# Matmul with batch norm over rows: x cast in GpSimd DMAs and transposed on VectorE, column tiles finished one after another

One core of a Trainium2 chip. The metric is the time of one execution in device microseconds; the profile's span runs from the first to the last instruction and is some 2 us shorter.

## The reference

```python
x: (16, 512, 1024) fp32     weight: (1024, 768) fp32     gamma, beta: (768,)
y = np.matmul(x, weight)                        # 8192 x 768
mean = np.mean(y, axis=(0, 1)); var = np.var(y, axis=(0, 1))
return gamma * (y - mean) / np.sqrt(var + eps) + beta
```

The statistics of a column need all 8192 rows of it, so no element of a column can be finished before its last row is multiplied. But columns do not depend on one another: that is what the change uses.

## The kernel before

Rows come in 16 chunks of 512, columns in six tiles of 128, the contraction in eight pieces of 128. y^T of all chunks stays in SBUF as bf16.

```python
for mt in range(M_T):                       # 16 chunks
    x_sb = xpool.tile([P, M_SUB, K], f32)
    nc.sync.dma_start(x_sb, ...)            # 2 MB, rows of 4 KB
    nc.scalar.copy(x_bf, x_sb)              # cast to bf16
    for kt in range(K_T):                   # 32 transposes of 128x128 on TensorE
        for ms in range(M_SUB):
            nc.tensor.transpose(psum_t[:, ms, :], x_bf[:, ms, kt*P:(kt+1)*P], ident)
        nc.scalar.copy(xT_sb[:, kt, :], psum_t)
    for nt in range(N_T):
        for kt in range(K_T):
            nc.tensor.matmul(py, w_sb[:, kt, nt*P:(nt+1)*P], xT_sb[:, kt, :], ...)
        nc.vector.bn_stats(stats_sb[:, nt, mt, :], py)
        nc.vector.tensor_copy(yT_sb[:, nt, m0:m0 + M_CHUNK], py)
# ... aggregate statistics, scale and shift of all 768 columns ...
for mt in range(M_T):
    for nt in range(N_T):
        nc.scalar.activation(yn, yT_sb[...], Identity, bias=shift, scale=scale)
        for ms in range(M_SUB):
            nc.tensor.transpose(opsum[:, ms, :], yn[:, ms*P:(ms+1)*P], ident)
        nc.vector.tensor_copy(o_sb, opsum)
        nc.sync.dma_start(out[...], o_sb)   # 256 KB, rows of 512 bytes, three buffers
```

## Time and profile before

| | before |
|---|---|
| median of 3 runs before the prediction | 353.72 us (353.66 to 353.81) |
| start, TensorE without work | 0 to 20 us |
| matmuls and input transposes | 20 to 236 us, TensorE clock 1.00 |
| output stage | 240 to 352 us, clock 0.50, DMA share 0.79 |

The slices behind this table are shown in the prediction; the last two rows are these stretches, with the columns of the prediction's table of stretches:

```profile
20.00:236.00 216.00, 203.99 (x1256) 104.89 (x1280) 123.60 (x195) 121.97 (x145) 0.00 (x0) 1.00 0.38 138
...
240.00:352.00 112.00, 56.23 (x384) 40.04 (x384) 66.26 (x96) 75.65 (x96) 0.00 (x0) 0.50 0.79 226
```

In the line of slices each digit is the busy share of one fortieth of the span in tenths. In a group, the figures after the bar are total busy time and the mean of one in ns, then the idle time of the engine just ahead of them and what ended it. A 512-column matmul is recorded with 380 ns, but the next starts 216 ns after it. Costs of matmuls are therefore read from start to start.

### The profile page before, as it was taken

To read this page: it belongs to the slowest core of one execution; us is meant where nothing else is said; L and a number is where in the kernel's file an instruction comes from. 1 tells how busy PE (TensorE), PEld (TensorE's weight loads), DVE (VectorE), ACT (ScalarE), POOL (GpSimd) and SP (SyncE) were. 2 spreads that over 40 slices of the span, in tenths; PEclk is the share of its full clock that TensorE was granted. 3 is DMA by queue.
4 is the path that set the end of the run, shared out by engine and by line. 5 is a ranking of instruction groups with operands and counts; after the bars stand their busy time and mean duration, and the time that the engine had idled before them with its cause. 6 is when DMAs were issued, how large, how long until landed. Compare 5 with 4: busy or idle time off the path is not lost.

```text
span 352.2 us, 4346 instructions
## 1 busy us (share of the span) xinstructions
PE 260.5 (74%) x1640; PEld 144.9 (41%) x1664; DVE 196.1 (56%) x300; ACT 203.1 (58%) x243; POOL 0.7 (0%) x6
## 2 busy tenths in 40 slices
PE   0059999999999999999999999984554555455542
PEld 0034554544544544544544544533333334333331
DVE  0306556556565565465475475495664666566653
ACT  1196835835835736736736633607775777577751
POOL 0000000000000000000000000000000000000000
PEclk9999999999999999999999999995555555555555
DMA  7999563363372362462460000004886888688867
GB/s 288 409 342 325 187 238 102 138 239 98 143 240 81 159 238 72 168 238 50 190 238 2 0 2 1 2 0 114 245 245 199 243 243 255 180 249 240 254 194 208
DMA packets 61925, 62.16 MB, mean 176 GB/s; under 512 B 3536, under 2 KB 52688, under 8 KB 61904
## 3 DMA queue, kind: packets, MB, share of 16 engines
q1 hardware_dynamic: 61904, 61.88, 53.6%
q8 instruction: 13, 0.21, 0.3%
q14 instruction: 8, 0.07, 0.1%
HBM read 36.71 MB, written 25.17 MB: 176 GB/s over the span
## 4 chain that ended last, share of the span: by engine, by line
PE 47%; DMA 27%; ACT 13%; DVE 10%; issue 2%; DVEq 0%; SPq 0%; ACTq 0%
PE py L87 42%; DMA out_dram<-o_sb 22%; ACT xT_sb L82 11%; DVE o_sb L134 7%; PE psum_t L77 5%; DMA x_sb<-in_x_dram 4%; ACT x_bf L71 2%; DVE yT_sb L95 1%; DVE stats_sb L94 1%; DVE mv_sb L99 1%; DVEq L134 0%; ACT yn L124 0%; PE opsum L132 0%; SPq L55 0%; ACT tmp L114 0%
## 5 line engine op out<-in xcount | busy, mean ns | idle before, releaser
L87 PE MATMUL py<-xT_sb,w_sb 128*128 128x512 bf16 x744 | 178.8, 380 | 1.6 <-ACT xT_sb L82 1.1
L94 DVE BATCH_NORM_STATS2 stats_sb<-py 128x6 f32<-128x512 f32 x96 | 66.8, 696 | 97.4 <-PE py L87 97.3
L82 ACT COPY xT_sb<-psum_t 128x512 bf16<-128x512 bf16 x128 | 67.9, 586 | 86.8 <-PE psum_t L77 86.8
L87 PEld LDWEIGHTS <-w_sb 128*128 128x128 bf16 x768 | 74.6, 98 | 80.0 <-issue 5.0
L132 PE MATMUL opsum<-ident,yn 128*128 128x128 bf16 x384 | 56.2, 300 | 54.7 <-DVE o_sb L134 49.3
L124 ACT ACTIVATE yn<-yT_sb,shift_sb,scale_sb 128x512 bf16<-128x512 bf16 x96 | 76.2, 811 | 30.2 <-PE opsum L132 26.4
L134 DVE CAST o_sb<-opsum 128x512 f32<-128x512 bf16 x96 | 66.3, 691 | 43.2 <-DMA out_dram<-o_sb 31.3
L77 PE MATMUL psum_t<-ident,x_bf 128*128 128x128 bf16 x512 | 47.4, 220 | 30.4 <-ACT x_bf L71 20.4
L132 PEld LDWEIGHTS <-yn 128*128 128x128 bf16 x384 | 40.0, 137 | 71.1 <-issue 64.9
L71 ACT CAST x_bf<-x_sb 128x4096 bf16<-128x4096 f32 x16 | 57.7, 3608 | 14.7 <-DMA x_sb<-in_x_dram 14.7
L95 DVE CAST yT_sb<-py 128x512 bf16<-128x512 f32 x96 | 64.6, 673 | 0.0
L77 PEld LDWEIGHTS <-x_bf 128*128 128x128 bf16 x512 | 37.6, 98 | 51.0 <-issue 26.9
L57 DVE CAST w_sb<-w_tmp 128x6144 bf16<-128x6144 f32 x1 | 3.4, 3359 | 10.8 <-DMA w_tmp<-in_weight_dram 10.8
L114 ACT ACTIVATE tmp<-mv_sb,eps_sb 128x6 f32<-128x6 f32 x1 | 0.3, 299 | 9.3 <-DVE mv_sb L99 9.3
L99 DVE BATCH_NORM_AGGREGATE mv_sb<-stats_sb 128x2 f32<-128x96 f32 x6 | 3.5, 578 | 0.0
L71 ACT ACT_TABLE_LOAD x1 | 1.3, 1283 | 0.7 <-PEq L155 0.7
L114 ACT ACT_TABLE_LOAD x1 | 1.3, 1283 | 0.0
L113 DVE MEMSET eps_sb<- 128x1 f32 x1 | 0.1, 59 | 0.8 <-PEq L155 0.8
L115 DVE RECIPROCAL scale_sb<-tmp 128x6 f32<-128x6 f32 x1 | 0.2, 191 | 0.4 <-ACT tmp L114 0.4
masks.py:199 POOL TENSOR_SCALAR_AFFINE_SELECT ident<-ident 128x128 bf16<-128x128 bf16 x1 | 0.3, 292 | 0.1
L116 DVE TENSOR_TENSOR scale_sb<-scale_sb,gamma_sb 128x6 f32<-128x6 f32 x1 | 0.2, 167 | 0.1
masks.py:197 POOL MEMSET ident<- 128x128 bf16 x1 | 0.2, 205 | 0.3 <-POOLq L155 0.3
(6 smaller groups left out, 0.7 us busy)
## 6 DMA issues: line engine op xcount, KB each, us to landing
x_sb<-in_x_dram SPq DMA_DIRECT2D x16, 2048.0 KB, 7.8
out_dram<-o_sb SPq DMA_DIRECT2D x96, 256.0 KB, 2.4
w_tmp<-in_weight_dram SPq DMA_DIRECT2D x1, 3072.0 KB, 10.9
gamma_sb<-in_gamma_dram SPq DMA_DIRECT2D x6, 0.5 KB, 7.6
beta_sb<-in_beta_dram SPq DMA_DIRECT2D x6, 0.5 KB, 7.2
```

Of the source, the lines that this page charges most:

```text
L57: nc.vector.tensor_copy(w_sb, w_tmp)
L71: nc.scalar.copy(x_bf, x_sb)
L77: nc.tensor.transpose(psum_t[:, ms, :], x_bf[:, ms, kt * P:(kt + 1) * P], ident,)
L82: nc.scalar.copy(xT_sb[:, kt, :], psum_t)
L87: nc.tensor.matmul(py, w_sb[:, kt, nt * P:(nt + 1) * P], xT_sb[:, kt, :], start=(kt == 0), stop=(kt == K_T - 1),)
L94: nc.vector.bn_stats(stats_sb[:, nt, mt, :], py)
L95: nc.vector.tensor_copy(yT_sb[:, nt, m0:m0 + M_CHUNK], py)
L99: nc.vector.bn_aggr(mv_sb[:, nt, :], stats_sb[:, nt, :, :])
L114: nc.scalar.activation(tmp, var, mybir.ActivationFunctionType.Sqrt, bias=eps_sb, scale=1.0)
L124: nc.scalar.activation(yn, yT_sb[:, nt, m0:m0 + M_CHUNK], mybir.ActivationFunctionType.Identity, bias=shift_sb[:, nt:nt + 1], scale=scale_ ...
L132: nc.tensor.transpose(opsum[:, ms, :], yn[:, ms * P:(ms + 1) * P], ident)
L134: nc.vector.tensor_copy(o_sb, opsum)
```

## The change

The intent is to take everything but matmuls off TensorE's path, and to write output while TensorE still multiplies:

- x comes through casting DMAs as bf16 (of the weights one half too, the other half as fp32 through the hardware queue). VectorE transposes 32x32 blocks of *pairs* of bf16, taken as one fp32 word; the rows of the weights are permuted so that the contraction still matches. A matmul then reads every second bf16 of the pairs.
- x^T of chunks 4 to 15 stays in SBUF. All six column tiles are computed for chunks 0 to 3, three tiles for the rest; these three are then complete, and their output runs beside the matmuls of tile 3, and so on. These three are stored together, in rows of 1.5 KB; each later tile alone, in rows of 512 bytes.
- Output transposes stand one behind each matmul, what is left of a bank just before its copy. Evacuation of y moves from VectorE to ScalarE, normalization from ScalarE to VectorE.
- 26 dummy matmuls run at the start, the schedule is laid out by planned times in the code, and each engine's order is pinned to it.

```diff
-        nc.sync.dma_start(x_sb, x_flat[...])
-        nc.scalar.copy(x_bf, x_sb)
-                nc.tensor.transpose(psum_t[:, ms, :], x_bf[...], ident)
-            nc.scalar.copy(xT_sb[:, kt, :], psum_t)
+        for i in range(4):                                  # load_x, 256 rows
+            seq(nc.gpsimd.dma_start(x_bf[32 * i:32 * i + 32], rows[:, :, KQ * i:KQ * (i + 1)]))
+        src = xs[q].rearrange("p t k -> p (t k)").bitcast(f32)   # turn_x
...
+        seq(nc.vector.transpose(dst[:, half, :, jw0:jw1], src[:, :, jw0:jw1]))
...
+                seq(nc.tensor.matmul(                       # mm: eight per unit
+                    y_ps, w_sb[:, jw, e, nt * P:(nt + 1) * P], xT[c][:, jw, :, e], ...))
+                if turns:
+                    turn_one()                              # one output transpose
...
+    for c in range(2, C):
+        for nt in range(NT if c < EARLY else GA):           # EARLY = 4, GA = 3
+            unit(nt, c, MM_US)
+    at(pe + 1.9, finish, ga)
+    outputs(ga, pe + 6.0, 2.24, 2, 2)
+    for nt in range(GA, NT):
+        for c in range(EARLY, C):
+            unit(nt, c, MM_US + (1.05 if nt == GA else 0.35))
+        at(pe + 1.9, finish, [nt])
+        outputs([nt], pe + 7.0, 2.3 if nt < NT - 1 else 1.0, 8, 1)
```

The cuts leave out the pools, the start with chunks 0 and 1 in halves, the statistics, and the rest of the schedule.

## The prediction

> **What bounds the kernel now.** I read the page first, then a table of stretches, then the tensor engine's own timeline in one steady stretch. From the page, the slices, the chain of work that ended last, and four groups:
>
> ```profile
> span 352.2 us, 4346 instructions
> ...
> PE   0059999999999999999999999984554555455542
> ...
> PEclk9999999999999999999999999995555555555555
> DMA  7999563363372362462460000004886888688867
> ...
> PE 47%; DMA 27%; ACT 13%; DVE 10%; issue 2%; DVEq 0%; SPq 0%; ACTq 0%
> ...
> L87 PE MATMUL py<-xT_sb,w_sb 128*128 128x512 bf16 x744 | 178.8, 380 | 1.6 <-ACT xT_sb L82 1.1
> ...
> L82 ACT COPY xT_sb<-psum_t 128x512 bf16<-128x512 bf16 x128 | 67.9, 586 | 86.8 <-PE psum_t L77 86.8
> ...
> L134 DVE CAST o_sb<-opsum 128x512 f32<-128x512 bf16 x96 | 66.3, 691 | 43.2 <-DMA out_dram<-o_sb 31.3
> ...
> out_dram<-o_sb SPq DMA_DIRECT2D x96, 256.0 KB, 2.4
> ```
>
> There are three stages. For 20 us (slices 1 and 2) the tensor engine (PE) waits for data. Until about 236 us it is over 90% busy at full clock while DMA is used by a third and falls to 0. Then comes a stage at half clock in which DMA is 80% busy and PE half: the writing of the output. The stages follow each other because the statistics need all of y before any output can be normalized. The table of stretches puts numbers on this:
>
> ```profile
> 2.00:12.00 10.00, 0.00 (x0) 0.00 (x0) 0.38 (x1) 0.01 (x1) 0.00 (x0) 1.00 1.00 381
> 12.00:20.00 8.00, 0.00 (x0) 0.00 (x0) 2.98 (x1) 3.31 (x1) 0.00 (x0) 1.00 1.02 410
> ...
> 245.00:300.00 55.00, 29.08 (x200) 20.91 (x199) 34.50 (x50) 39.78 (x51) 0.00 (x0) 0.50 0.82 236
> ```
>
> After the length come the busy times of PE, weight loads, VectorE, ScalarE and GpSimd, then granted clock, DMA share and GB/s. Loads run at 381 to 410 GB/s with DMA full; stores of 512-byte rows do 236 GB/s at a share of 0.82, so about 288 if the queue never ran dry. It runs dry because only three output buffers circulate (31.3 us of waits of L134 on the store).
>
> The PE timeline between 100 and 128 us gives the costs:
>
> ```profile
> 106.95 9.22 PE L87 MATMUL py<-xT_sb,w_sb 128*128 128x512 bf16 x42 [0.18 <-ACT xT_sb L82]
> 116.02 0.61 PE L77 MATMUL psum_t<-ident,x_bf 128*128 128x128 bf16 x8
> 117.13 0.38 PE L77 MATMUL psum_t<-ident,x_bf 128*128 128x128 bf16 x4 [0.51 <-ACT xT_sb L82]
> ```
>
> A 512-column matmul costs (9.22 - 0.38)/41 = 0.2156 us, start to start (the 380 ns of the group is latency). A transpose costs (0.61 - 0.38)/4 = 0.0575 us. A chunk of 512 rows takes 116.02 - 102.67 = 13.35 us: 48 matmuls 10.35, 32 transposes 1.84, the remaining 1.2 waits for ScalarE's copies of x^T. So 768 matmuls are 165.6 us that nothing here removes; about 187 us of the span are start, input transposes, waits, and the output stage.
>
> **What the Trainium skill says.**
> - "DMA: Bandwidth & Descriptors", section "SWDGE vs HWDGE vs iDMA": a casting DMA must come from GpSimd, and its descriptors are written by software there. The kernel before has only hardware queues, so its trace shows no rate for this. It is the largest unknown.
> - "SBUF — State Buffer", section "SBUF: two separate sides": a VectorE operation in a two-port mode locks GpSimd out, and such DMAs starve. Not visible before. The change seems written with this in mind: while x loads, VectorE does transposes and statistics from PSUM; the normalizations from SBUF to SBUF come after the last load.
> - "TensorE: Matmul & The Clock Gate", section "Part 4: PE-mode transpose": transposes do not count as activity for the clock. The trace agrees: 0.50 granted in the stage that has only transposes, 1.00 before it.
> - "Vector Engine (DVE) Microarchitecture Reference", section "3.8 The reshape front-end and per-opcode configuration": the 32x32 transpose passes one element per cycle and lane. No run here shows it yet.
>
> **The change part by part.**
>
> *Loads.* x arrives as bf16 through 128 GpSimd DMAs, four per 256 rows, in 1 KB reads and 512-byte writes. Removed: 16 casts of 3.6 us on ScalarE. I assume 385 GB/s read (the low end of 381 to 410), so 2.7 us per 256 rows. Two words of bf16 are treated as one fp32, and VectorE transposes 32x32 blocks of such pairs: 32 transposes of 1024 words. Statistics over 512 elements take 0.65 us here, a 6-element operation 0.17, so I estimate 0.17 + 2 x 0.48 = 1.1 to 1.2 us each, 38 us in all. That takes 512 transposes (29 us) off PE and 128 copies (68 us) off ScalarE. VectorE also loses 96 casts (65 us), which move to ScalarE as copies of about 0.57.
>
> *Order on PE*, as the built program has it: 26 dummy matmuls, chunks 0 and 1 with half-width pieces, all six column tiles for chunks 0 to 3, three tiles for the rest; then the statistics of those three are complete, and their output work (192 transposes) goes between the matmuls of tile 3, and so on. x^T stays in SBUF for this. Of 384 output transposes, 312 stand before the last matmul, and 72 after it (8 of tile 4, 64 of tile 5).
>
> *The sum, in span time:*
> 1. Weights and the first two x pieces are 5.24 MB: 13.6 us at 385 GB/s, plus 1.5 to start and about 2 to land: 17. The second half of chunk 0 is 24 matmuls, 5.2 us: 22.3. Chunk 1: 48 x 0.2156 = 10.4: 33.
> 2. Twelve units of eight matmuls for chunks 2 and 3, 36 for the rest: 48 x 1.725 = 82.8: 116. The last x piece lands at about 17 + 30 x 2.7 + 3 = 101 and is needed at about 110, so loads are hidden by 9 us.
> 3. 36 units of the last three tiles: 62.1, and 312 transposes x 0.0575 = 17.9: 196.
> 4. Waits for banks and buffers: 1.2 us per chunk before; fewer handoffs now, I take 4 in all: 200.
> 5. Tail to the first store: last statistics, aggregate, square root, four small operations took 239.40 - 236.36 = 3.0 before, of which 0.6 was a cast now elsewhere: 2.5. Two normalizations 0.5, eight transposes at half clock 1.0, one copy of 1024 elements 1.1: 205.
> 6. Eight stores of 512 KB, 4.19 MB, at about 275 GB/s (below the 288, above the 236, for four larger buffers circulate): 15.3. First byte and final landing 2.5: 223.
> 7. Time over span was 353.72 - 352.2 = 1.5: about 224.
>
> Check of DMA: after 126 us, 12.6 MB in rows of 1.5 KB (say 350 GB/s, between 512-byte stores and 4 KB loads: 36 us) and twice 4.19 MB (15 us each): until 192, just ahead of the tail. ScalarE in that stage: per block of 512 rows two copies of 768 elements, (0.586 x 1.4) = 0.8 each, and about 0.5 of a copy from the matmuls, 2.1 us out of some 2.3. Both fit, narrowly, so I add 3 for collisions: **227 us**.
>
> **The rivals.**
> *Software descriptors bound the loads.* If a GpSimd DMA costs 1 us instead of 0.68, 256 rows take 4 us, the last x piece lands at about 140, and everything after step 2 moves by 30 us: about 255. For: the count of 128 DMAs with small rows, no trace. Against: the schedule in the code is laid out for 2.7 us, like a number once measured.
> *Stores or ScalarE bind from 126 us on.* Store rows of 1.5 KB at 288 GB/s need 44 us, not 36; copies in program order would then hold up ScalarE's evacuations and PE. That adds 5 to 12 us: 232 to 239. For: the two narrow margins. Against: slack of some 8 us before the tail.
> *PE loses by mixing.* The moving operand now steps over every second bf16, and each transpose stands between two matmuls. If either slowed 512-column matmuls by 10%, 17 us are added: 244. The trace speaks against a cost of switching: the transposes at 116.02 begin 9.07 after 106.95, which is 42 x 0.2156. Of the step it shows nothing.
> *All hidden, no gain* would need the 92 us of output stage to remain exposed. Five sixths of it now run beside matmuls, so I give it little.
>
> **Range and chances.** The best case has no collisions, and stores at 288: 218. Moderate slowness of the loads or of the stores gives 235 to 243. So 227, 8 in 10 between 218 and 243. Even the rivals added up stay below 310, so faster by over 2% has 0.97, within 2% 0.02, slower 0.01.
>
> **What would show it.** Right: PE clock 1.00 from the first real matmul to about 200 us; PE over 90% busy from about 23 to 200; 512-column matmuls 0.216 apart, with 0.27 where a transpose stands between; x transposes of 1.1 to 1.2 us; the last x landing near 101; a tail of 22 to 25 us with DMA full; no waits of PE on x after chunk 1. Wrong: long waits of VectorE's transposes for x (the first rival), waits of ScalarE's output copies on stores with a PE waiting for banks (the second), a matmul spacing above 0.22 before any output transpose (the third), or a start later than 23 us.

## The result

| | before | after |
|---|---|---|
| median, 4 runs each | 353.7 us | 233.99 us (233.37 to 234.68) |
| ratio | | 0.6613 (95%: 0.6599 to 0.6626) |
| span of the profiled run | 352.2 us | 231.8 us |

The ratio compares runs of both kernels and is not quite the ratio of the medians. 234 lies inside the predicted 218 to 243, 7 us above the predicted 227.

The page of the changed kernel, the slices and the groups that answer to those of before:

```profile
span 231.8 us, 3336 instructions
...
PE   7649999999999999999999999999999999994800
...
PEclk9967999999999999999999999999999999997665
DMA  7999999999999999999000059999989932786898
...
L167 PE MATMUL y_ps<-xT_sb,w_sb 128*128 128x512 bf16 x672 | 166.3, 387 | 0.0
...
L149 POOL DMA_DIRECT2D x_bf<-in_x_dram x128 | 73.3, 578 | 21.6 <-issue 6.2
...
L160 DVE STREAM_TRANSPOSE xT_sb<-x_bf 128x1024 f32<-128x1024 f32 (+1 forms) x34 | 39.6, 1173 | 28.7 <-DMA x_bf<-in_x_dram 28.1
```

TensorE is busy from slice 4 to slice 36 with no idle time ahead of its 672 main matmuls (0.0, where before it also waited for ScalarE's copies of x^T). After slice 4 the clock does not fall before the tail. DMA now has work in two stretches: x until about 110 us, output from 134 us. The dip in PEclk in slices 3 and 4 is new. TensorE's timeline gives the milestones:

```profile
1.23 8.46 PE L127 MATMUL idle_ps<-idle_sb 128*128 128x512 bf16 x26 [1.23 <-DVE idle_sb L82]
14.29 0.37 PE L137 MATMUL y_ps<-xT_sb,w_sb 128*128 128x256 bf16 x1 [4.61 <-DVE xT_sb L160]
...
39.35 92.63 PE L167 MATMUL y_ps<-xT_sb,w_sb 128*128 128x512 bf16 x408
131.83 0.59 PE L208 MATMUL o_ps<-ident,y_sb 128*128 128x128 bf16 x6
132.25 0.39 PE L167 MATMUL y_ps<-xT_sb,w_sb 128*128 128x512 bf16 x1
132.48 0.22 PE L208 MATMUL o_ps<-ident,y_sb 128*128 128x128 bf16 x1
132.53 0.39 PE L167 MATMUL y_ps<-xT_sb,w_sb 128*128 128x512 bf16 x1
```

Chunk 1 ends at 39.35 us. Then 408 matmuls take 131.83 - 39.35 = 92.48 us: **0.2267 us each, not 0.2156**, at full clock and before any output transpose. A matmul and its transpose take 0.28 (132.25 to 132.53), so the transpose adds some 0.055, no more than it costs in a row of transposes. The last matmul ends at about 208.9, the first store of the last tile can start at 214.7, and the end is at 231.8.

### The profile page after: what moved, and what is told of

Read it like the earlier page. It is cut to its first block, busy times and chain, and to the rows that moved or that the text cites. A ratio compares the mean times of both kernels' runs of the same rounds, so it can differ in the third digit from the quotient of the medians.

```text
span 231.8 us, 3336 instructions
## 1 busy us (share of the span) xinstructions
PE 209.7 (90%) x1238; PEld 107.3 (46%) x1238; DVE 142.9 (62%) x256; ACT 102.2 (44%) x156; POOL 82.7 (36%) x150
## 3 DMA queue, kind: packets, MB, share of 16 engines
q1 hardware_dynamic: 33792, 26.74, 37.3%
## 5 line engine op out<-in xcount | busy, mean ns | idle before, releaser
L167 PE MATMUL y_ps<-xT_sb,w_sb 128*128 128x512 bf16 x672 | 166.3, 387 | 0.0
L180 ACT CAST y_sb<-y_ps 128x512 bf16<-128x512 f32 x96 | 56.5, 588 | 83.7 <-DVE stats L175 83.5
L175 DVE BATCH_NORM_STATS2 stats<-y_ps 128x6 f32<-128x512 f32 x96 | 64.3, 685 | 43.5 <-PE y_ps L167 33.8
L149 POOL DMA_DIRECT2D x_bf<-in_x_dram x128 | 73.3, 578 | 21.6 <-issue 6.2
L208 PE MATMUL o_ps<-ident,y_sb 128*128 128x128 bf16 x384 | 61.3, 230 | 3.7 <-DVE y_sb L193 3.6
L160 DVE STREAM_TRANSPOSE xT_sb<-x_bf 128x1024 f32<-128x1024 f32 (+1 forms) x34 | 39.6, 1173 | 28.7 <-DMA x_bf<-in_x_dram 28.1
L218 ACT CAST o_sb<-o_ps 128x768 f32<-128x768 bf16 (+1 forms) x52 | 45.3, 883 | 25.7 <-ACT y_sb L180 9.6
L208 PEld LDWEIGHTS <-y_sb 128*128 128x128 bf16 x384 | 33.5, 103 | 7.4 <-DVE y_sb L193 4.4
L193 DVE TENSOR_SCALAR y_sb<-y_sb,scale,shift 128x512 bf16<-128x512 bf16 x96 | 33.4, 404 | 0.0
L137 PE MATMUL y_ps<-xT_sb,w_sb 128*128 128x256 bf16 (+1 forms) x156 | 24.5, 321 | 5.4 <-DVE xT_sb L160 4.6
```

The source lines that it names most:

```text
L137: seq(nc.tensor.matmul(py[nt, c][:, q0 * QR:q1 * QR], w_sb[:, jw, e, nt * P:(nt + 1) * P], xT[c][:, jw, q0 * QR:q1 * QR, e], start=(jw == ...
L149: seq(nc.gpsimd.dma_start(x_bf[32 * i:32 * i + 32], rows[:, :, KQ * i:KQ * (i + 1)]))
L160: seq(nc.vector.transpose(dst[:, half, :, jw0:jw1], src[:, :, jw0:jw1]))
L167: seq(nc.tensor.matmul(y_ps, w_sb[:, jw, e, nt * P:(nt + 1) * P], xT[c][:, jw, :, e], start=(jw == 0 and e == 0), stop=(jw == JW - 1 and e ...
L175: seq(nc.vector.bn_stats(stats[:, nt, c, :], py[nt, c]))
L180: seq(nc.scalar.copy(y_sb, py.pop((nt, c))))
```

## The experiments

Eleven kernels ran. The first is the changed kernel unaltered, the reference for the others.

> The changed kernel again, unaltered, so that the three runs beside it have a reference on the same chip: 234 us within 1 us, 512-column matmuls 0.2267 us apart before the first output transpose, chunk 1 finished at 39 us.

Measured: 233.53 us, ratio 0.6602 (0.6584 to 0.6620), chunk 1 finished at 39.03 us, the last matmul at about 208.6. As expected.

### 1. Adjacent operands (wrong result)

```diff
-                    y_ps, w_sb[:, jw, e, nt*P:(nt+1)*P], xT[c][:, jw, :, e],
+                    y_ps, w_sb[:, jw, e, nt*P:(nt+1)*P],
+                    xT[c][:, jw].rearrange("p m e -> p (m e)")[:, e*CH:(e+1)*CH],
```

> Every matmul reads 512 adjacent bf16 of x^T in place of every second one; the result is wrong on purpose, the instructions and their number stay. Theory A (the step over every second element slows the matmul by 5%): spacing falls from 0.2267 to 0.2156 us, the value of the kernel before; 768 matmuls x 0.0111 = 8.5 us less, 225.5 us. Theory B (something beside the matmul slows it, such as DMA or VectorE traffic, or the alternation of banks): spacing stays 0.2267 and the time 234.

Measured: 227.11 us, ratio 0.6418 (0.6409 to 0.6427). TensorE's timeline:

```profile
39.83 88.22 PE L167 MATMUL y_ps<-xT_sb,w_sb 128*128 128x512 bf16 x399
127.89 0.85 PE L208 MATMUL o_ps<-ident,y_sb 128*128 128x128 bf16 x6
```

The same 408 matmuls (a few records are missing) take 127.89 - 39.83 = 88.06 us, 0.2158 each. Theory A holds: every other instruction, transfer and engine is the same, and the spacing goes back to the value of before. The total falls by 6.4 in place of 8.5 us: the 672 main matmuls give 7.3, but in the first chunks TensorE waits for x instead, and chunk 1 ends at 39.83 in place of 39.03.

### 2. More dummy matmuls

```diff
-    WAKE = 26
+    WAKE = 46
```

> 46 dummy matmuls in place of 26, so that the tensor engine is busy until about 14.0 us, when the first real one can start. Theory A (the 4.6 us gap before the first real matmul put the clock to 0.50 until 20 us, and that half-speed stretch is on the path): the clock stays 1.00 from 14 us, the first 48 pieces take 5.2 us in place of 7.8, and chunk 1 ends 2 to 3 us earlier; total about 231.5. Theory B (the late arrival of the second half of the weights sets the start, whatever the clock): the tensor engine waits for weights near 20 us instead, and the total stays within 0.5 us of 234.

Measured: 232.03 us, ratio 0.6562 (0.6535 to 0.6588). The table of stretches (length, TensorE busy, clock, DMA share, GB/s), first of the changed kernel, then of this run:

```profile
15.40:20.00 4.60, 4.58 (x22) 0.50 1.19 185
20.00:23.00 3.00, 3.00 (x15) 0.95 1.41 188
```
```profile
15.40:20.00 4.60, 3.88 (x28) 1.00 1.08 170
20.00:23.00 3.00, 3.00 (x15) 1.00 1.40 183
```

The first two lines are from the profile in "The result": after a gap of 4.6 us ahead of the first real matmul the clock is 0.50 until 20 us. (In the unaltered kernel the gap is 5.5 us, and the first stretch has 0.58.) With 46 dummies the gap is 2.0 us and the clock stays at 1.00. Chunk 1 ends at 37.76 in place of 39.03, the last matmul 1.3 us earlier. So the half-speed stretch was on the path, but only for 1.3 us and not the 2 to 3 that I expected, since TensorE then waits for data (busy 3.88 of 4.60). In total the intervals of the two ratios touch, so the run times alone would not prove a gain.

### 3. All output last

```diff
-    EARLY = 4
+    EARLY = C          # all six tiles for all chunks, then all statistics, then all output
```

Its x loads from chunk 4 on are paced to the matmuls, since x^T has 6 buffers here.

> The finishing of column tiles in turn is undone: all six tiles for all 16 chunks, then the statistics of all, then all output. The x loads from chunk 4 on are laid out at the pace of the matmuls, as x^T then has 6 buffers. If the overlap of output with matmuls is most of the gain: last matmul at 39.4 + 672 x 0.2267 = 192 us, then 6 us to the first store, 12.6 MB at some 363 GB/s (35 us) and 12.6 MB at some 270 (47 us): about 280 to 283. If the gain came mostly from the input side, the total would stay below 250.

Measured: 283.29 us, ratio 0.8002 (0.7989 to 0.8015); span 281.3. Stretches, with the columns of the first table in the prediction:

```profile
39.00:191.00 152.00, 151.08 (x659) 64.38 (x671) 86.64 (x110) 50.02 (x86) 56.55 (x100) 1.00 0.64 80
200.00:235.00 35.00, 22.01 (x246) 18.51 (x244) 23.34 (x73) 24.52 (x33) 0.00 (x0) 0.74 1.02 360
235.00:280.00 45.00, 13.76 (x112) 11.55 (x111) 8.77 (x16) 17.21 (x17) 0.00 (x0) 0.50 1.03 281
```

The gain of 120 us therefore splits in two: 70 (353.6 to 283.3) without any overlap of output, and 50 (283.3 to 233.5) from the overlap. The 50 can be recounted. After the last matmul (191.4) the output takes 281.3 - 191.4 = 89.9 us; in the unaltered kernel 231.2 - 208.6 = 22.6. That is 67 us less, for 17 us of output transposes that now stand ahead of the last matmul. The two stretches of output also show the stores' rates with DMA full: 360 GB/s for rows of 1.5 KB, 281 for rows of 512 bytes.

The 70 can be recounted too. Chunks 2 to 15 took 14 x 13.35 = 186.9 us before and take 191.4 - 39.0 = 152.4 here, 34.5 less: 25.8 are input transposes gone from TensorE (14 x 1.84), 16.2 its waits for ScalarE's copies (14 x 1.16), and 7.5 go back to the slower matmuls (672 x 0.0111). Up to the end of chunk 1 it is 10 us less (49.3 to 39.0). The output stage is 26 us shorter (116 from 236.2 to 352.2, now 89.9): DMA is full, where before it was used by 0.79, and half of the bytes go in longer rows. By the two rates above, 12.6 MB at 360 in place of 281 GB/s are some 10 of the 26 us, an estimate.

This run also shows something of the clock. From 196.6 us on TensorE has nothing but transposes (slices 29 to 40 of 7 us):

```profile
PE   8389999999999999999999999992955754520250
...
PEclk9869999999999999999999999997795595555555
```

The clock is 0.50 while they run back to back at first (20 in 2.37 us from 196.5), 1.00 from 200.5 to 210.5 (68 in 4.42 us of work from 201), 0.50 from 211 to 224, and 1.00 again from 224.5 to 230. So the prediction's reading of the kernel before, that a stage of transposes alone has the clock at 0.50 because they do not count as activity, doesn't hold in general: there TensorE was also busy for only 56.23 of 112 us. What raises the clock here and lowers it again is not shown.

### 4. Output transposes in bursts

```diff
-                if turns:
-                    turn_one()
```

> The output transposes are no longer dealt out one behind each matmul; the six or eight of one bank run together just before their copy. Theory A (a transpose costs 0.056 us wherever it stands, so placing them between matmuls gains nothing in itself; what gains is that the stage overlaps): within 1 us of 233.5, pairs gone, the same last matmul at 209 us. Theory B (interleaving hides the transposes' weight loads or spares waits for VectorE's normalization): the last matmul comes 3 us or more later, 237 or above.

Measured: 234.76 us, ratio 0.6643 (0.6623 to 0.6663), the last matmul within 0.6 us of the unaltered kernel's. TensorE's timeline:

```profile
131.81 1.97 PE L167 MATMUL y_ps<-xT_sb,w_sb 128*128 128x512 bf16 x8
133.61 0.83 PE L206 MATMUL o_ps<-ident,y_sb 128*128 128x128 bf16 x12
134.28 1.97 PE L167 MATMUL y_ps<-xT_sb,w_sb 128*128 128x512 bf16 x8
```

Twelve transposes take 134.28 - 133.61 = 0.67 us, 0.056 each, as in pairs. Theory A holds: "output transposes between matmuls" as one-by-one interleaving is worth nothing to TensorE. The 1.2 us more, just outside the 1 us expected, arises behind the last matmul (first transposes of the last tile at 213.2 in place of 212.2), as 16 and not 8 transposes of tile 4 are left for then.

### 5. Twice as many DMAs for x

```diff
-            seq(nc.gpsimd.dma_start(x_bf[32*i:32*i+32], rows[:, :, KQ*i:KQ*(i+1)]))
+            for h in range(0, QT, QT // 2):
+                seq(nc.gpsimd.dma_start(x_bf[32*i:32*i+32, h:h+QT//2], rows[:, h:h+QT//2, KQ*i:KQ*(i+1)]))
```

> Each GpSimd DMA of x is split in two: 256 DMAs of 128 descriptors in place of 128 of 256, the same bytes. Theory A (0.575 us is paid per DMA, and eight may be in flight): 8 x 0.575 = 4.6 us for 256 rows in place of 3.1, the last x piece transposed at about 30 + 26 x 4.6 = 150 in place of 110 us, some 9 us of slack used up and the rest exposed: 255 to 265 us, with the tensor engine waiting for x. Theory B (the cost goes with the descriptors): 0.29 us each, the time stays at 233 to 235.

Measured: 275.44 us, ratio 0.7794 (0.7782 to 0.7806). From GpSimd's instructions of that line (count: duration ns min/median/max):

```profile
L150 POOL DMA_DIRECT2D x_bf<-in_x_dram x256: 542/542/694, 1.3 to 156.0; - x128
```

Half the descriptors, and yet 542 ns in place of 575. The cost is per DMA, as in theory A; the 0.29 us of theory B are refuted. The last x piece is transposed at 159.6 us in place of 109.2 in the unaltered kernel, 50 us later, and the total grows by 42: some 7 to 8 us of slack were used up first (by the two profiles 7), where the prediction had 9. TensorE itself hardly waits for x (2.3 us), but 26.9 us for ScalarE's evacuations. These stand behind statistics, and the statistics stand in VectorE's order behind transposes that wait 73.1 us for x. The total is larger than the 255 to 265 of the expectation because GpSimd also stood still for 16 us, which I had left out. This is the prediction's first rival, made real: the changed kernel lies one such step from it.

### 6. The casting DMA alone, in the kernel before

```diff
-        nc.sync.dma_start(x_sb, ...)
-        nc.scalar.copy(x_bf, x_sb)
+        nc.gpsimd.dma_start(x_bf, ...)
```

> The kernel before, with one part of the change alone: x arrives as bf16 through 16 GpSimd DMAs of 512 rows, and ScalarE's 16 casts of 3.6 us go. Transposes stay on the tensor engine. Theory A (the 1.2 us per chunk that the tensor engine waits are ScalarE's copies coming late behind the cast): 16 x 1.2 = 19 us less, and 3 to 4 us at the start: 330 us, chunks of 12.2 us. Theory B (they are the two transpose banks, whatever ScalarE does besides): chunks stay at 13.35 and only the start gains: 349 to 351.

Measured: 351.66 us, ratio 0.9944 (0.9932 to 0.9957). A chunk still takes 113.55 - 100.21 = 13.34 us:

```profile
100.21 0.61 PE L74 MATMUL psum_t<-ident,x_bf 128*128 128x128 bf16 x8
101.32 0.38 PE L74 MATMUL psum_t<-ident,x_bf 128*128 128x128 bf16 x4 [0.50 <-ACT xT_sb L79]
...
113.55 0.61 PE L74 MATMUL psum_t<-ident,x_bf 128*128 128x128 bf16 x8
```

Theory B, though the total is 0.7 us above its 351: 58 us of ScalarE's time go, and the wait behind the first eight transposes stays at 0.50 us, because it is the copy of just those transposes out of two banks. What frees TensorE in the change is that the transposes leave it, not that the cast leaves ScalarE.

### 7. Transposes of single bf16, 46 dummies

```diff
-        src = xs[q].rearrange("p t k -> p (t k)").bitcast(f32)   # and so on, in pairs
+        src = xs[q].rearrange("p t (b c) -> p t b c", c=32)
+        dst = xT[c].rearrange("p jw e (q t r) -> p q t (jw e) r", q=QPC, r=32)
-        rows = weight.rearrange("(i jw c e) n -> i c jw (e n)", i=4, jw=JW, e=2)
+        rows = weight.rearrange("(i jw e c) n -> i c jw e n", i=4, jw=JW, e=2)
...
```

> A correct way to adjacent moving operands: VectorE transposes single bf16 elements in 32x32 blocks (2048 per partition and piece, with the weights' rows permuted to suit) in place of pairs taken as fp32; 46 dummy matmuls as in the run before. Theory A (one element per cycle whatever its width): 2.3 us per piece in place of 1.24, VectorE needs 32 x 2.3 + 60 x 0.67 = 114 us before the first three tiles are done, about as long as the tensor engine (126 us), so part of the 7 us gained by the spacing of 0.2157 is lost to waits: 228 to 234. Theory B (the transpose goes by bytes): 1.2 us per piece, about 225.

Measured: correct, 231.37 us, ratio 0.6551 (0.6525 to 0.6577). Two groups:

```profile
L165 PE MATMUL y_ps<-xT_sb,w_sb 128*128 128x512 bf16 x672 | 160.3, 379 | 4.6 <-ACT y_sb L178 4.6
...
L158 DVE STREAM_TRANSPOSE xT_sb<-x_bf 128x2048 bf16<-128x2048 bf16 (+1 forms) x34 | 73.1, 2156 | 12.5 <-DMA x_bf<-in_x_dram 12.5
```

Theory A: a full piece of 2048 elements takes 2.28 us, one of 1024 words 1.24, and a half piece of 1024 bf16 elements 1.20: here the number of elements sets the time and not their width. Matmuls are back at 0.2158, now with a correct result (37.28 to 84.06 for 216 of them, with a last 0.38 taken off: 46.40/215), but VectorE is now busy for 60.00 of the 60 us from 60 to 120, evacuations come late behind its statistics, and TensorE stands idle 4.6 us. Of the 7 us to be had, little is left.

### 8. The step of two, put into the kernel before

```diff
-        xT_sb = xtpool.tile([P, K_T, M_CHUNK], bf16, tag="xt")
+        xT_sb = xtpool.tile([P, K_T, M_CHUNK, 2], bf16, tag="xt")    # read and written at [..., 0]
...
```

> The kernel before, with x^T written to every second bf16 of a tile twice as wide, and read from there (and the weights loaded in four pieces to make room); the result stays right. Theory A (the step alone makes a 512-column matmul 5% slower, in any kernel): runs of matmuls at 0.2267 us spacing in place of 0.2156, 768 x 0.0111 = 8.5 us more, about 362, somewhat less if the start gains from the four pieces. Theory B (the 5% belongs to the changed kernel's other traffic): spacing 0.2156, time 351 to 354.

Measured: 366.43 us, ratio 1.0360 (1.0337 to 1.0384).

```profile
111.05 9.65 PE L89 MATMUL py<-xT_sb,w_sb 128*128 128x512 bf16 x42 [0.23 <-ACT xT_sb L84]
120.53 0.61 PE L79 MATMUL psum_t<-ident,x_bf 128*128 128x128 bf16 x8
```

42 matmuls start over 120.53 - 111.05 = 9.48 us, 0.2257 each, against 0.2156. So the step slows matmuls in an otherwise different kernel as well: theory A, from both sides. The total rose by 12.7 and not 8.5: ScalarE's copies into every second element also became slower (mean 733 ns, 586 before), and TensorE waits 0.65 in place of 0.51 us for the first of them in a chunk. A chunk takes 120.53 - 106.17 = 14.36 us, 1.01 more than before, of which the matmuls are 0.48; an earlier start gives a part back.

### 9. Six tiles for five chunks, on top of experiment 7

```diff
-    EARLY = 4
+    EARLY = 5
-                at(t + 2.0, cast_w, n)
+                at(6.0 if n == 0 else t + 2.0, cast_w, n)
```

> The run with single-bf16 transposes, with all six column tiles for five chunks in place of four (three more units for the tensor engine early, so that VectorE is less behind), and VectorE's cast of the first weights put ahead of its first transposes. If VectorE's 2.28 us transposes are what made the tensor engine wait 4.6 us between 60 and 120 us, these waits fall below 1.5 us, and the cast saves 1.2 us at the start: about 227. If the three extra units only move the end of the first three tiles, 231.

Measured: correct, 230.31 us, ratio 0.6525 (0.6502 to 0.6548). TensorE still waits 4.8 us for evacuations between 84 and 119 us, so my guess about the extra units failed; 231 was the right expectation. The earlier cast gained nothing either: chunk 1 ends at 37.28 as in experiment 7. That VectorE's long transposes cause the waits is thus argued from the trace (VectorE is busy for all 81 us from 39 to 120) and not shown by this run. Its median is the lowest of a correct kernel here, though its interval overlaps that of experiment 7. The medians say 1.4% below the unaltered change, and the intervals of the two ratios do not overlap, but they were taken in different calls.

### 10. All weights through the hardware queue

```diff
-    order = [("x", 0), ("f", 0), ("x", 1), ("f", 1), ("w", 2, 4)]
+    order = [("x", 0), ("f", 0), ("x", 1), ("f", 1), ("f", 2), ("f", 3)]
...
```

> The kernel with 46 dummy matmuls and pair transposes, the first weight cast ahead, and all of w through the hardware queue in fp32 with casts on ScalarE and VectorE, so that GpSimd's eight DMAs in flight serve x alone. If GpSimd's wait for earlier landings (2.9 us twice before 14 us) delays the second half of the weights, chunk 1 ends 2 to 4 us before the 37.8 of the run with 46 dummies: 228 to 230. If bytes bound the start, chunk 1 ends at 37 or later and the time stays at 231 to 232.

The expectation is wrong about its base: it was built on experiment 9 (single bf16, five chunks), not on pairs, so it is compared with that. Measured: 238.89 us, ratio 0.6753 (0.6744 to 0.6762), 8.6 us more. TensorE's timeline:

```profile
17.32 2.52 PE L137 MATMUL y_ps<-xT_sb,w_sb 128*128 128x256 bf16 x12 [4.69 <-DVE xT_sb L158]
23.33 2.72 PE L137 MATMUL y_ps<-xT_sb,w_sb 128*128 128x256 bf16 x12 [3.48 <-DVE xT_sb L158]
```

The first x pieces land later (TensorE begins at 17.3 in place of 14.9), chunk 1 ends at 46.5 in place of 37.3. Both expectations failed. The first eight DMAs of x are issued by 6.03 us in both runs, before GpSimd waits for anything; yet the second piece, which they bring, is transposed from 22.0 us in place of 16.4. So with all weights in flight at once x gets a smaller part of DMA, at a time when x is needed first. How much of the rest is GpSimd's wait for earlier landings stays open.

## Why the prediction was right, and where it was off

The mechanism held from chunk 1 on: matmuls without idle time, the output of five tiles beside them, and the tail of the sixth. By its own steps, in span time:

| step | predicted | measured | difference |
|---|---|---|---|
| 1. end of chunk 1 | 33 | 39.35 | +6.3 |
| 2, 3. 84 units of eight matmuls | 144.9 | 152.3 (672 x 0.2267) | +7.4 |
| 3. 312 transposes | 17.9 | 17.2 | -0.7 |
| 4. waits for banks and buffers | 4 | 0 | -4 |
| 5. last matmul to first store | 5 | 5.8 | +0.8 |
| 6. stores of the last tile | 17.8 | 17.1 | -0.7 |
| 7. time over span | 1.5 | 2.2 | +0.7 |
| collisions added at the end | 3 | none seen | -3 |

The differences add up to 6.8, the 7 us between 227 and 234. That they are no more is luck: steps 1 and 2 were short by 13.7 us, and the 7 us set aside for waits and collisions, which did not occur, made good one half of it.

Of the signs it named for being right, these came: no waits of TensorE on x after chunk 1, 0.28 where a transpose stands between matmuls, a tail of 22.9 us. These did not: the clock at 1.00 from the first real matmul, a spacing of 0.216, the last x near 101. One sign of being wrong came: a spacing above 0.22 before any output transpose.

- **The third rival was real, at half the size I gave it.** I had written that the trace shows nothing of the step over every second bf16, and left it out of the sum. It costs 5%, shown from both sides by experiments 1 and 8. The other half of that rival, a cost of mixing transposes with matmuls, did not occur (experiment 4).
- **The start was sized too small.** My sum counted bytes at 385 GB/s. The first x piece was transposed only from 13.5 us. From 15.4 us TensorE works without a pause: chunks 0 and 1 are worth 96 matmuls, 21.8 us at 0.2267, and the half clock until 20 us adds some 2.3 to that (estimates from these figures). My sum had the first 24 of them, 5.2 us, done by the time the data had come at 17 us. That is the term that failed. GpSimd issued eight DMAs by 6.06 us and then stood still for 2.9 us:

```profile
1.30 4.76 POOL L149 DMA_DIRECT2D x_bf<-in_x_dram  x8 [0.85 <-POOLq L343]
8.96 0.54 POOL L109 DMA_DIRECT2D w_sb<-in_weight_dram  x1 [2.90 <-DMA x_bf<-in_x_dram]
```

  The ninth starts 0.28 us after the first has landed (8.68), and in the traces of five of these kernels no GpSimd DMA starts before the landing of the one eight before it: no more than eight are in flight. I had not looked for that. With the half clock gone, only 1.3 us are won, as the data then bind (experiment 2). What each of these is worth alone is argued, not shown.
- **Loads were hidden, as predicted.** The last x piece was transposed at 110 and not 101, the matmuls also came later, and some slack remained: experiment 5 used up 7 to 8 us of it. Whether some VectorE operations would starve these loads, which the prediction considered, no run here tests.
- **The second rival did not occur.** Output from 134 to 170 us ran at 329 GB/s on average beside the matmuls, and TensorE had no wait for it.
- **Transposes on VectorE** took 1.24 us against 1.1 to 1.2, normalizations 0.40 against 0.25: both off the path until the tail. Most of the 0.8 us in step 5 is the square root, which starts 0.55 us after its input (210.95 against 210.40) because ScalarE is still copying.
- **Chances.** "Faster" with 0.97 was safe: with all output exposed (experiment 3) the kernel is still 70 us faster, and of these 26 lie in the output stage itself, the rest on the input side.

## What to carry to other kernels

When a reduction separates two stages, look for the dimension that it does not cross: finishing column tiles in turn hid nearly five sixths of the output and was worth 50 of 120 us, while the placing of single transposes between matmuls was worth nothing. Taking work off an engine helps only if that work is on the path: 58 us of casts taken from ScalarE alone gave 0.6%. And before a layout trick feeds the busiest engine, measure that engine on the new access pattern: a step of two cost 5% of every matmul. Without it VectorE's transposes took nearly twice as long and became the limit (experiment 7), so little was won.

## What the Trainium skill lacked or had wrong

- "SBUF — State Buffer", section "Door 1: The DMA port swizzle (why `[64,N]` ≈ `[32,N]`)": it says that how far one can stride for free depends on the type, up to 8 elements for bf16, with at least two hits on a 16-byte line. For TensorE's moving operand a step of 2 is not free: 0.2267 us per 512-column matmul against 0.2158 with adjacent elements, and 0.2257 against 0.2156 in the other kernel.
- "DMA: Bandwidth & Descriptors", section "SWDGE vs HWDGE vs iDMA": it gives no issue cost of a casting DMA. Here GpSimd spends 0.575 us on one of 256 rows of 1 KB, 0.542 on one of half as many and 0.74 on one of 512 rows of 4 KB (experiment 6), so nearly all of it is per DMA.
- "DMA: Bandwidth & Descriptors", section "Specifications": 512 bytes are given as enough for line rate. Stores with DMA full moved 281 GB/s with rows of 512 bytes and 360 GB/s with rows of 1.5 KB.
- "TensorE: Matmul & The Clock Gate", section "Part 4: PE-mode transpose": it says that the full clock does not engage for transposes. The output stage before agrees (0.50 throughout), experiment 3 does not: with transposes alone the clock was 1.00 from 200.5 to 210.5 us. Nor do transposes mixed with matmuls lower it (1.00 from 134 to 206 us in the changed kernel).
